# A hybrid encoder trunk on one core: the state-space branch written right behind its projection, beside the last gate

## The chip, the cores and the metric

The kernel runs on one core of one Trainium2 chip. The core has five engines, each with its own queue: TensorE (PE) for matmuls, VectorE (DVE) and ScalarE (ACT) for elementwise work, GpSimd (POOL) and SyncE (SP), which here mostly issue DMAs. The metric is the device time of one execution in microseconds; lower is better.

## The reference, cut to what matters

Two layers, each on 1024 tokens of width 1024. One projection of the normalised input feeds four branches of width 256:

- A, a convolution module: gated linear unit, causal depthwise convolution with 31 taps, LayerNorm, swish, a 256 by 256 matmul.
- B, a gated linear recurrence in chunks.
- C, a state-space branch: a causal convolution with 4 taps on x, B and C (768 columns), then a chunked scan:

```python
xbc = silu(causal_depthwise_conv(xbc, conv_w, conv_b))
a_cs = cumsum(a, axis=chunk)                     # a = dt * -exp(a_log)
scores = (C @ B.T) * masked_exp(causal, seg)     # seg: differences of a_cs
y = scores @ xdt + (C @ state) * exp(a_cs) + xs * d_skip
state = exp(a_cs_last) * state + B.T @ wx        # handed to the next chunk
y = rms_norm(y * silu(z))
```

- D, latent attention: a projection to a query latent (256), a key/value latent (128) and a rotary key (32), norms, up-projections, block-causal softmax.

A and D are multiplied by a SiLU gate of their own, B and C too (C's is z). One 1024 by 1024 output projection, a norm and the residual close the layer.

## The kernel before, in words

Matmuls of the large projections run in a two-part float32 format: each operand is split into a high and a low part ("wh"/"wl" for weights, "hh"/"hl" for the input), and each product is three matmuls (lines 209 to 211, 220 to 226, 347 to 349).

Each piece of a layer is a Python generator ("thread") that writes some instructions and yields how many units of work they were. The table PLAN gives each thread a start, an end and a total on a common scale; `weave` (line 262) always advances the thread whose position on that scale is lowest:

```python
def pos(self):
    return self.start + self.span * self.done / self.total
...
t = min(threads, key=Thread.pos)
w = next(t.gen, None)
```

So PLAN decides only the order in which instructions are written, and the numbers in it are places in that order, not times of the chip. The framework then lays out each engine's queue: an instruction that is written earlier goes first, but one whose inputs are there may pass earlier ones that are still waiting. Each engine then works through its queue in order. Tiles come from pools with a fixed number of slots per tag; a tile that finds no free slot waits for the release of an earlier one. The tags that matter here:

- `smA`, 2 accumulators of one bank: the gates' `psg` and `psgA`, the convolution tail's `ptA`, `pt2A`, `pyA`, and the state update `pstC` of branch C (line 31, 115 to 117). `smB`, 2: `ptx`, `pcb`, `pyC` of C, `pq` and `ptq` of the queries. `big`, 2 of two banks: `psx` (projection of x, B, C), `psd` and `pk` of D.
- `blk`, 19 slots of 128x544: x, B, C after their convolution hold 12 of them (6 per half of the tokens), the convolution of A holds 4 (`ca`), D wants 16 (`kT` 8, `cqT` 4, `vD` 4).
- `t2k`, 4 slots: `gtA` of the last gates, `lm` of C, later `pT` of attention. `t15`, 2 slots: `cn`, `kk` of D and `qk` of the queries. `k4`, 7 slots: gate tiles `gl`, `hnA`, `hsA`, and two of D's weight parts. Weights pass through `raw` (2 slots, DMAs from SP), `wh` and `wl` (3 each).

The threads around the change, for the first layer (keys end in 0; the second layer's end in 1):

- `x0`, th_x (line 700): projection of x, B, C in feature layout, then the 4-tap convolution on DVE (line 719) and SiLU (line 720).
- `ca0`/`cb0`, th_conv (line 473): branch A's 120 tap instructions on DVE (line 481), the first 57 on one line of the plan, the other 63 on another.
- `at0`, th_atail (line 485): its LayerNorm by transposes, pointwise matmul (line 515) and gate.
- `gd0`, gate_f(9, 1) (line 338): D's gate, four groups of 24 matmuls into `psgA`, each closed by a SiLU on ACT (line 353) and a DMA to DRAM.
- `c0`, th_c (line 724): branch C, eight chunks of 128 tokens. A chunk loads its decay row `lm` by a DMA from POOL (735), adds the mask (736), takes four exponentials on ACT (738), transposes (742), makes `pcb` (753), multiplies it into `lm` (754), makes `pyC` (760, 764) and hands the state on through `pstC` (774 to 778). Two chunks' halves end in a norm (789) and a DMA (365).
- `d0`, th_d (line 797): D's projection and keys, eight rows from the last token block to the first. A row is 24 matmuls into `psd`, a copy, three transposes (832), `pk` (841), scaling, four transposes (854) and copies to `kT`.
- `q0`: the first two query rows. Attention (`att0`) and the loading of the output weights (`w0`, line 948) are written after D's end; the output weights take the space of the layer's input, which is free once D's last `psd` is done.

The order in the trace is: B's levels, x's projection, D's gate, then C, A's tail and D's rows together, then attention and the output projection.

Of the kernel before, what the change touches and what calls it, by code (L numbers as in the profile page):

```python
# [47 lines left out]
    "fq0": (60.4, 110.8, 41),  # L48
    "dt0": (104, 115.8, 9),
    "ca0": (53.6, 123, 57),  # L50
    "cb0": (123, 300.5, 63),
    "gb0": (138.1, 155.9, 21),
    "b0": (123.3, 232.4, 120),
    "ga0": (151.5, 181.4, 21),
    "gc0": (203.4, 226.9, 21),
    "gd0": (278.8, 298.3, 21),
    "x0": (220.7, 257, 61.5),
    "at0": (296.3, 363.8, 22),
    "c0": (293.2, 362.4, 48.2),
    "d0": (283.6, 373.2, 72),  # L60
    "q0": (357.3, 375.6, 2),
    "o0": (482.2, 511, 8.2),
    "rot0": (221.2, 266.5, 1),
# [4 lines left out]
    "fq1": (59, 99.6, 41),  # L68
    "dt1": (104, 115.8, 9),
    "ca1": (57, 110, 44),  # L70
    "cb1": (110, 284.5, 76),
    "gb1": (117.9, 137.7, 21),
    "b1": (102.3, 200.5, 120),
    "ga1": (130.9, 155.3, 21),
    "gc1": (203.4, 230.3, 21),
    "gd1": (261.8, 280.6, 21),
    "x1": (212.9, 255.7, 61.5),
    "at1": (278.6, 342, 22),
    "c1": (275.5, 340.6, 48.2),
    "d1": (266.1, 351.4, 72),  # L80
    "q1": (335.5, 349.5, 2),
    "o1": (479.4, 508.2, 8.2),
    "att1": (347.1, 481.6, 144.8),
# [1084 lines left out]
```

## Time and profile before

| | us |
|---|---|
| median of three runs | 1263.75 (1263.0 to 1267.15) |
| the profiled execution, its own time | 1263.69 |
| its span in the trace | 1261.9 |
| PE busy | 1197.7 (95%) |
| DVE busy | 836.2 (66%) |
| ACT busy | 478.5 (38%) |
| chain that ended last, share of PE | 76% |
| chain that ended last, share of DVE | 14% |

Busy time of PE counts a matmul until its modelled end; a matmul that follows at once starts before that end. So a PE that is shown as busy may still be waiting a little between matmuls.

### The profile page before, as it was taken

The page shows a single profiled execution, that of the slowest core. Times are in us where ns is not written, and L with a number is a line of the kernel's source. Part 1 is how long each engine was busy: PE and PEld are TensorE (multiplying, and loading weights), DVE is VectorE, ACT ScalarE, POOL GpSimd, SP SyncE. Part 2 cuts the span into 40 slices and gives each one's busy share as a digit, 9 for nine tenths or more (in the row PEclk, how much of TensorE's full clock was granted, in tenths as well). Part 3 has the DMA queues.
Part 4 walks back from the last instruction along what each step waited for, and adds up shares of the span by engine and source line. Part 5 has one row for each costly group of instructions (what it writes and reads, how often), then busy time and mean ns, then how long its engine had stood idle before and what let it go on. Part 6 is the DMA issues. An engine that isn't in the chain of part 4 may idle for free.

```text
span 1261.9 us, 17853 instructions
## 1 busy us (share of the span) xinstructions
PE 1197.7 (95%) x6902; PEld 987.0 (78%) x6902; DVE 836.2 (66%) x1579; ACT 478.5 (38%) x1088; POOL 183.1 (15%) x290
## 2 busy tenths in 40 slices
PE   5999999899989989999999999998999998999997
PEld 5988899888878746678898889897888776566886
DVE  5566999985376386745454859999754763867232
ACT  5413322233474374433432222321435644644211
POOL 2100011201133111210020001211012322112000
PEclk9999999999999989989999999998999899999999
DMA  7001122201151040244221111211114311202531
GB/s 274 34 34 68 44 83 85 76 34 48 62 156 61 22 153 23 66 148 147 101 97 67 34 51 59 92 52 67 35 61 123 106 36 54 93 18 68 188 129 71
DMA packets 38660, 101.47 MB, mean 80 GB/s; under 512 B 5440, under 2 KB 13808, under 8 KB 38576
## 3 DMA queue, kind: packets, MB, share of 16 engines
q1 hardware_dynamic: 22848, 51.42, 11.9%
q0 software_dynamic: 14864, 46.04, 11.1%
q10 hardware_dynamic: 864, 2.88, 0.6%
q8 instruction: 54, 0.88, 0.3%
q14 instruction: 30, 0.25, 0.1%
HBM read 75.37 MB, written 25.20 MB: 80 GB/s over the span
## 4 chain that ended last, share of the span: by engine, by line
PE 76%; DVE 14%; ACT 3%; DMA 3%; issue 2%; POOL 0%; DVEq 0%; POOLq 0%; ACTq 0%
PE pz L991 13%; PE psx L220 4%; PE psx L223 4%; PE psx L226 4%; PE psc L909 3%; DVE ca L481 3%; PE plB L625 2%; PE psA L220 2%; PE psA L223 2%; PE psA L226 2%; PE poD L927 2%; PE ptp L923 2%; PE psgA L347 2%; PE psgA L348 2%; PE psgA L349 2%
## 5 line engine op out<-in xcount | busy, mean ns | idle before, releaser
L481 DVE SCALAR_TENSOR_TENSOR ca<-hpad,col,ca 128x512 f32<-128x512 f32 x240 | 186.3, 782 | 3.9
L176 DVE TENSOR_TENSOR wl<-raw,wh 128x1024 fp32r<-128x1024 f32 (+2 forms) x56 | 66.9, 1195 | 92.0 <-ACT wh L160 91.9
L160 ACT CAST wh<-raw 128x1024 fp32r<-128x1024 f32 (+2 forms) x56 | 57.5, 1027 | 139.8 <-PE psA L223 33.7
L991 PE MATMUL pz<-woh,yh 128*128 128x512 f32 x240 | 78.2, 405 | 0.2 <-ACT yh L160 0.2
L991 PE MATMUL pz<-woh,yl 128*128 128x512 f32 x240 | 75.7, 397 | 0.0
L991 PE MATMUL pz<-wol,yh 128*128 128x512 f32 x240 | 75.7, 397 | 0.0
L209 PE MATMUL psg<-wh,hh 128*128 128x256 f32 x256 | 73.9, 289 | 1.5 <-ACT gt L160 1.4
L909 PE MATMUL psc<-kT,qTt 96*128 96x512 f32 (+4 forms) x192 | 73.2, 505 | 0.9 <-ACT pe L914 0.8
L210 PE MATMUL psg<-wl,hh 128*128 128x256 f32 x256 | 73.2, 286 | 0.0
L211 PE MATMUL psg<-wh,hl 128*128 128x256 f32 x256 | 72.8, 284 | 0.0
L914 ACT ACTIVATE pe<-psc,nm 128x1024 f32<-128x1024 f32 (+7 forms) x64 | 47.2, 739 | 64.3 <-DVE nm L912 63.8
L625 PE MATMUL plB<-qz,krb 128*128 128x128 f32 x448 | 63.0, 288 | 8.5 <-DVE krb L635 8.5
L625 PEld LDWEIGHTS plB<-qz,krb 128*128 128x128 f32 x448 | 58.3, 200 | 10.7 <-issue 5.5
L220 PE MATMUL psx<-hh,wh 128*128 128x512 f32 x192 | 62.3, 403 | 0.0
L719 DVE SCALAR_TENSOR_TENSOR xbc<-xpad,col,xbc 128x512 f32<-128x512 f32 x72 | 51.1, 748 | 16.3 <-ACT xbc L172 15.5
L223 PE MATMUL psx<-hl,wh 128*128 128x512 f32 x192 | 61.7, 401 | 0.0
L226 PE MATMUL psx<-hh,wl 128*128 128x512 f32 x192 | 61.1, 397 | 0.0
L991 PEld LDWEIGHTS pz<-wol,yh 128*128 128x128 f32 x240 | 45.6, 190 | 10.6
L176 DVE TENSOR_TENSOR yl<-yt,yh 128x512 fp32r<-128x512 f32 x16 | 11.0, 690 | 64.7 <-ACT yh L160 64.7
L912 DVE TENSOR_REDUCE nm<-psc 128x1 f32<-128x1024 f32 (+7 forms) x64 | 47.2, 745 | 9.9 <-PE psc L909 9.9
L991 PEld LDWEIGHTS pz<-woh,yl 128*128 128x128 f32 x240 | 45.3, 189 | 10.6 <-issue 0.2
L991 PEld LDWEIGHTS pz<-woh,yh 128*128 128x128 f32 x240 | 44.9, 190 | 9.8 <-ACT yh L160 0.4
(331 smaller groups left out, 3052.3 us busy)
## 6 DMA issues: line engine op xcount, KB each, us to landing
raw<-in_w_dram SPq DMA_DIRECT2D x44, 512.0 KB, 3.4
rawo<-in_wo_dram SPq DMA_DIRECT2D x16, 512.0 KB, 4.1
gsp<-gt POOLq DMA_DIRECT2D x16, 256.0 KB, 2.5
gl<-gsp POOLq DMA_DIRECT2D x8, 512.0 KB, 5.0
gspF<-gtA POOLq DMA_DIRECT2D x16, 256.0 KB, 2.3
ysp<-gl POOLq DMA_DIRECT2D x8, 512.0 KB, 3.4
lm<-acsp POOLq DMA_DIRECT2D x16, 256.0 KB, 4.0
yt<-ysp SPq DMA_DIRECT2D x16, 256.0 KB, 3.4
```

The lines of the kernel that those rows point to most:

```text
L160: (V.tensor_copy if name in ONV else A.copy)(out_, in_)
L176: V.tensor_tensor(lo, src, hi.bitcast(F32), op=ALU.subtract)
L209: T.matmul(ps[:, :n], a, hs[k], start=(k == 0), stop=False)
L210: T.matmul(ps[:, :n], a, ls[k], start=False, stop=False)
L211: T.matmul(ps[:, :n], b, hs[k], start=False, stop=(k == KD - 1))
L220: T.matmul(ps[:, h * 512:(h + 1) * 512], w, hh[:, k, h * 512:(h + 1) * 512], start=(k == 0), stop=False)
L223: T.matmul(ps[:, h * 512:(h + 1) * 512], w, hl[:, k, h * 512:(h + 1) * 512], start=False, stop=False)
L226: T.matmul(ps[:, h * 512:(h + 1) * 512], wl, hh[:, k, h * 512:(h + 1) * 512], start=False, stop=(k == KD - 1))
L481: V.scalar_tensor_tensor(t, hp[:, k:k + 512], w[k], t, op0=ALU.mult, op1=ALU.add)
L625: T.matmul(pl[:, o0:o0 + P].rearrange("p (r b u) -> p r b u", r=2, u=u), k_[:, t_ * P:(t_ + 1) * P], z[:, :, t_ * P:(t_ + 1) * P].rearrang ...
L909: T.matmul(psc[:, c0:c1_], qTt[0:k_, h, :], kT[h, c0 // 512][0:k_, 0:c1_ - c0], start=True, stop=True)
L991: T.matmul(pz[n], a[:, k, :], w[:, k, n * 512:(n + 1) * 512], start=(k == 0 and a is yh and w is wh), stop=(k == KD - 1 and a is yl))
```

## The change

Ten lines of PLAN, five per layer; no generator is touched. On the plan's scale, x ends at 257 in the first layer and 255.7 in the second, before and after. C's start moves from 293.2 to 260 and from 275.5 to 258; D's gate starts at 268 (was 278.8) and 256 (was 261.8); the end of A's convolution moves from 300.5 to 285 and from 284.5 to 272; A's tail starts 9.3 and 4.6 places earlier; D's projection starts 4.4 and 3.9 places later and ends where it did.

```diff
-    "cb0": (123, 300.5, 63),
+    "cb0": (123, 285, 63),
-    "gd0": (278.8, 298.3, 21),
+    "gd0": (268, 292, 21),
-    "at0": (296.3, 363.8, 22),
-    "c0": (293.2, 362.4, 48.2),
-    "d0": (283.6, 373.2, 72),
+    "at0": (287, 358, 22),
+    "c0": (260, 350, 48.2),
+    "d0": (288, 373.2, 72),
...
-    "cb1": (110, 284.5, 76),
+    "cb1": (110, 272, 76),
-    "gd1": (261.8, 280.6, 21),
+    "gd1": (256, 278, 21),
-    "at1": (278.6, 342, 22),
-    "c1": (275.5, 340.6, 48.2),
-    "d1": (266.1, 351.4, 72),
+    "at1": (274, 336, 22),
+    "c1": (258, 334, 48.2),
+    "d1": (270, 351.4, 72),
```

## Rows read from the trace of the kernel before

**Rows 1.** The page, part 1: busy time, share of the span and instructions by engine.
```profile
PE 1197.7 (95%) x6902; PEld 987.0 (78%) x6902; DVE 836.2 (66%) x1579; ACT 478.5 (38%) x1088; POOL 183.1 (15%) x290
```

**Rows 2.** Windows, first layer, from gate D's start: length, busy by engine, clock, DMA.
```profile
326.02:349.22 23.20, 23.20 (x103) 19.04 (x102) 6.99 (x9) 10.68 (x17) 4.33 (x8) 1.00 0.26 80
349.22:375.00 25.78, 22.12 (x143) 19.00 (x142) 20.69 (x59) 21.79 (x64) 8.04 (x13) 1.00 0.55 177
375.00:415.70 40.70, 38.55 (x231) 32.37 (x230) 28.03 (x97) 18.65 (x69) 12.81 (x21) 1.00 0.15 47
415.70:440.23 24.53, 22.42 (x121) 19.12 (x120) 5.79 (x27) 8.23 (x31) 3.31 (x6) 1.00 0.08 28
440.23:452.00 11.77, 7.78 (x22) 4.27 (x21) 9.43 (x23) 9.11 (x22) 5.14 (x5) 0.74 0.40 118
```

**Rows 3.** Windows, second layer, behind gate D.
```profile
970.40:996.00 25.60, 23.07 (x132) 19.67 (x131) 20.43 (x58) 20.14 (x56) 8.04 (x13) 0.87 0.55 179
996.00:1038.60 42.60, 40.65 (x242) 34.19 (x241) 28.24 (x97) 20.45 (x78) 12.18 (x20) 1.00 0.14 45
```

**Rows 4.** Timeline of PE inside gate D: start, length, line, tiles.
```profile
340.37 0.40 PE L347 MATMUL psgA<-hh,wh 128*128 128x512 f32 x1
340.61 0.40 PE L348 MATMUL psgA<-hl,wh 128*128 128x512 f32 x1
```

**Rows 5.** Timeline of PE, rows of C, D and the first query, in time order.
```profile
353.99 1.00 PE L760 MATMUL pyC<-xdt,lm 128*128 128x64 f32 x8
...
358.65 1.08 PE L760 MATMUL pyC<-xdt,lm 128*128 128x64 f32 x8 [0.58 <-DVE mvA L495]
...
424.16 1.11 PE L841 MATMUL pk<-kvt,ckT 128*128 128x512 f32 x2 [0.47 <-DVE kr L850]
...
432.05 1.12 PE L841 MATMUL pk<-kvt,ckT 128*128 128x512 f32 x2 [0.92 <-ACT kT L160]
433.01 0.60 PE L879 MATMUL ptq<-idn,qk 128*96 128x128 f32 x4
433.45 0.61 PE L753 MATMUL pcb<-xbc,xbc 128*128 128x128 f32 x4
```

**Rows 6.** Timeline of ACT: a gate's SiLU, a table load, D's last weights, a query.
```profile
331.81 0.60 ACT L353 ACTIVATE gtA<-psgA 128x512 f32<-128x512 f32 x1 [0.33 <-PE psgA L349]
...
339.11 1.28 ACT L1082 ACT_TABLE_LOAD   x1
340.40 1.28 ACT L738 ACTIVATE lm<-lm,nacs 128x128 f32<-128x128 f32 x4
...
352.76 0.89 ACT L160 CAST wh<-raw 128x832 fp32r<-128x832 f32 x1 [1.50 <-DMA raw<-in_wd_dram]
...
430.42 0.58 ACT L166 ACTIVATE qk<-pq,rq 128x384 f32<-128x384 f32 x1
```

**Rows 7.** Timeline of POOL: two of the four loads of D's first keys' mask rows.
```profile
331.49 0.53 POOL L811 DMA_DIRECT2D kT<-in_amask_dram  x1 [9.60 <-ACT xbc L720]
...
361.32 0.59 POOL L811 DMA_DIRECT2D kT<-in_amask_dram  x1
```

**Rows 8.** The page, part 6: DMA issue, count, size, median us to landing.
```profile
lm<-acsp POOLq DMA_DIRECT2D x16, 256.0 KB, 4.0
```

**Rows 9.** Windows of line 481 alone (A's taps), DVE busy and count.
```profile
60.00:240.00 180.00, 77.24 (x101) 1.00 0.17 61
...
680.00:860.00 180.00, 70.94 (x93) 1.00 0.17 61
```

**Rows 10.** Windows ahead of x's projection, both layers, as in Rows 2.
```profile
240.00:250.00 10.00, 6.41 (x46) 5.89 (x45) 10.00 (x17) 4.34 (x8) 0.72 (x1) 0.90 0.25 79
860.00:870.00 10.00, 5.48 (x22) 4.95 (x23) 10.00 (x17) 1.45 (x4) 0.71 (x1) 0.62 0.37 133
```

**Rows 11.** Timeline of DVE at D's end, first layer.
```profile
448.11 1.23 DVE L789 TENSOR_TENSOR gl<-gl,msc 128x1024 f32<-128x1024 f32 x1 [1.32 <-POOL msc L147]
...
450.39 0.28 DVE L160 COPY kT<-pk 96x128 f32<-96x128 f32 x1
```

## The prediction, made before the result was known

> **What bounds the kernel now.** I read the page's busy times first, then windows of each layer from gate D to attention, then the timelines of PE, ACT, POOL and DVE inside them. PE is busy for 95% of the span [rows 1], so no edit of the order can save much; what an order can change is the time in which PE has nothing to do. In the first layer [rows 2] gate D is solid: 23.20 us, PE idle 0, DVE 6.99 us and ACT 10.68 us busy. Behind it, where C, A's tail and D's rows run together, PE is idle for 25.78 - 22.12 = 3.66 us and then 40.70 - 38.55 = 2.15 us; in D's last rows 24.53 - 22.42 = 2.11 us; and at D's end 11.77 - 7.78 = 3.99 us with the clock at 0.74. The second layer repeats it [rows 3]: 2.53 us idle and 1.95 us, and in the first of these stretches the mean granted clock is 0.87. A clock that is either full (2.4 GHz) or half (1.2 GHz) and means 0.87 was at half for 26% of 25.60 us, 6.7 us, which takes away up to 3.3 us of PE.
>
> These idle times are a little too small: a gate matmul is drawn 0.40 us long and the next starts 0.24 us after it [rows 4], so each time PE runs dry some 0.16 us are hidden. With about ten such holes a layer that is 1.6 us more per layer, an estimate.
>
> What makes the holes is that three threads start cold at the same moment, right behind the gate: each is a chain across PE, DVE and ACT, and they wait for slots too. Of D's first four key tiles one is loaded at 331.49 us, after POOL waited 9.60 us for x's last SiLU to free a slot, and one only at 361.32 us [rows 7], when A's tail had given slots back. D's last weight part is cast at 352.76 us, 3.5 us behind the gate's end, having waited for its load [rows 6].
>
> **The change, part by part.** Its work is the same: no instruction is added but table loads, and each DMA is issued once as before. So I price waits.
>
> *C ahead of and beside gate D.* Written places: of gate D's 21 units 16 stood before C's first chunk; now three chunks stand among them in the first layer (from 260, 11.2 places a chunk, the gate ending at 292), two in the second. C needs x's last SiLU, so it can't run before about 332 us, but there it now goes first. PE pays for it in the gate: a 128-wide matmul takes (433.45 - 433.01) / 4 = 0.11 us [rows 5], a chunk has 24, so 2.6 us, some 8 us for three chunks. That lengthens the gate's stretch and shortens what follows by as much: zero by itself. What is won: of the 12 `blk` slots that x, B and C hold, 6 are given back after chunk 3, now earlier than D's rows want them, and behind the gate only two chains are cold instead of three. What stays is D's last weights, which will again be late by about 3.5 us, since their slots are freed by the gate's last group. The holes ahead of D's last rows come to 3.66 + 2.15 + 2.53 + 1.95 = 10.3 us, with 3.3 us of clock and 3.2 us hidden 16.8 us; bounds 0 and -16.8; I take half, -8.4, because the chain and slot half of them goes and the late weights and D's own waits stay.
>
> *The gate's accumulators.* This is the wait that is added. `smA` has two slots, handed out in written order; in the first layer C's state update `pstC` now stands before the gate's first group, and again before the third. One slot is thus held for C until x is through, and the gate's second group waits for the first group's SiLU: 0.33 + 0.60 us [rows 6], three times at most in the first layer and once in the second, 3.7 us. Behind the waiting matmul on PE stand only matmuls of C, which are written between. They fill most of it; I take +0.5 (bounds 0 and the third rival's +11).
>
> *ACT.* C's exponentials and the gate's SiLUs use different tables; the load takes 1.28 us and the exponential starts at its end, 340.40 against 339.11 + 1.28 [rows 6]. Two or three more alternations a layer make 5 to 8 us on an engine that was busy for 10.68 of 23.20 us, in a stretch that grows by 8 us: hidden, 0; without that cover it would land in the gate's hand-over and belongs to the third rival. The Trainium skill (ScalarE: Activation LUTs, What ACT_TABLE_LOAD costs) adds a drain of about 1.38 us to every switch, 2.66 us in all. This trace shows no such gap behind the load; by the skill's figure the alternations would cost 5 to 8 us at 2.66 / 1.28 times, 11 to 16 us of ACT; the stretch, 31 us with C's matmuls, still covers that, so the sum stays, and the gate's hand-over would be the more at risk.
>
> *A's convolution ends earlier.* It moves 3 to 4 taps of about 0.77 us [rows 9] ahead in the order, while B's chain makes PE wait 3.6 and 4.5 us [rows 10]. But the taps already run ahead of their place: 101 of 120 are done at 240 us [rows 9], and the 101st stands at place 244 before and 234 after, both behind B's end at 232; in the second layer the 93rd, done at 860 us, stands at 220 and 212, behind 200.5. They only fill gaps of DVE in both orders. I take 0; at worst 4 x 0.77 per layer, +6 in all.
>
> *A's tail a little earlier, D later.* POOL is passed by C's gate load, `lm` loads and zeroing of the state, which now go before D's key rows instead of behind the 9.60 us wait [rows 7]; SP keeps its order (x, gate, D). A's tail gives its `blk` slots back when the gate's last group frees `smA`, about as before: 0 (bounds -1 and +1).
>
> *D's last rows.* C's end moves from 362 to 350 while D ends at the same place, so D's last rows have less beside them. A row alone takes 432.05 - 424.16 = 7.89 us, with 0.47 or 0.92 us of waiting before `pk` [rows 5]. Two rows were nearly alone in the stretch with 2.11 us idle [rows 2], 1.06 us each, and with 0.16 us hidden at each of a row's two waits about 1.3 us; I count half a row more per layer, +1.3 (bounds 0 and two rows each, +5.2).
>
> *D's end.* C's eighth chunk was stuck: its `pcb` runs at 433.45 us, right behind the first query's `ptq`, which was written before it and held the place in `smB` until the query's scaling at 430.42 us found a slot of `t15` [rows 5, 6]. So C's last norm, 1.23 us on DVE, stood at 448.11 us in front of a copy of `kT` [rows 11] for which attention waits. Now C's end is written before the queries and is gone from there: -1.2 per layer, I take -2.1 in all (bounds 0 and -2.5).
>
> The sum: -8.4 + 0.5 + 0 + 0 + 0 + 1.3 - 2.1 = -8.7 us on the profiled execution's 1263.69, 1255.0 us. That execution equals the median shown (1263.75) within 0.1 us. I call a difference under 0.3%, 3.8 us, no change.
>
> **The rivals.** *The work is only moved* (no change). Gate D had no hole in PE, so the 8 us of C's matmuls now fill nothing there and are missing as filler later. For it: the total of matmuls is fixed, and D alone loses 1.3 us a row. Against it: the holes stood where all three threads were present, so filler wasn't what lacked. With two rows a layer more alone (+5.2) and a quarter of the holes closed (-4.2): -4.2 + 0.5 + 5.2 - 2.1 = -0.6: 1263.
>
> *All holes close* (more gain). The clock stays up in the second layer and the chains overlap wholly: -16.8 + 0.5 + 1.3 - 2.1 = -17: 1247. For it: C's fastest chunk takes 358.65 - 353.99 = 4.7 us [rows 5], less than a gate group (23.20 / 4 = 5.8 us). Against it: the late weights.
>
> *The gate waits for C* (slower). `smA` again: gate group 3 stands behind chunk 1's `pstC`. If a chunk needs its `lm` load (4.0 us [rows 8]), mask, table load and exponentials (1.28 + 1.28 us) one after the other, and the table is taken back for each SiLU (1.28), a chunk takes over 8 us against the gate's 5.8, and PE stops in the gate. It decides from the point where chunk 1's state update ends later than the gate's second group, some 13 us behind x's last SiLU. Price: hand-overs 3.7, then about 5 us of standing in the first layer and 2 in the second, 11 in all, less 2.1 at D's end: +9, 1273. Against it: the first two `lm` tiles have slots before the gate's own and can be ready ahead of x's end. The Trainium skill (Perfetto Trace Analysis, Optimization Strategy) reads a repeated gap on the saturated engine as too few slots for the next tile; gate D shows no such gap before, so this would be new.
>
> **How the numbers follow.** Forecast 0.50; only moved 0.21; all holes 0.12; gate waits 0.17. Faster: 0.50 + 0.12 = 0.62; same 0.21; slower 0.17. The forecast's own range is 1250 to 1259. The whole range goes down to 1244, past the all-holes case, and up to 1269, half-way into the slow one, which leaves out about 0.05 below and 0.12 above.
>
> **What would show it.** Right: in gate D's stretch PE stays busy with `ptx`, `pcb`, `pyC` of the first chunks between `psgA` groups, the fourth key row's load is issued before 355 us instead of at 361.32, the second layer's clock behind the gate is 1.00, and no norm of C stands behind D's end. Wrong: idle time of PE in front of `psgA` with the SiLU or the state update as releaser; holes of equal size in the stretch behind the gate; three or more D rows alone; or more than 3.6 and 4.5 us of idle PE ahead of x's projection, which would mean that A's taps do cost.

## The result, and the profile after

| | kernel before | changed kernel |
|---|---|---|
| median of four runs each, us | 1264.92 (1263.0 to 1267.15) | 1280.78 (1279.92 to 1281.77) |
| the profiled execution, us | 1263.69 | 1280.68 |
| its span, us | 1261.9 | 1278.5 |

The changed kernel is slower: ratio 1.0136, 95% interval 1.0118 to 1.0153. I had forecast 1255.0. The work is the same but for six more table loads on ACT; part 1 of the page after, against [rows 1]:

```profile
PE 1202.3 (94%) x6902; PEld 988.9 (77%) x6902; DVE 839.1 (66%) x1579; ACT 487.8 (38%) x1094; POOL 180.5 (14%) x290
```

PE is busy 4.6 us longer and the span is 16.6 us longer. Where that went is read best from one number per stage, which I work out from the matmuls of the trace: the length of a stretch less the sum, over its matmuls, of the spacing at which matmuls of that line and shape follow each other at full clock (the spacing that 15% of them undercut in the kernel before; 0.229 us for 512 columns, 0.109 for 128). It holds idle time, the holes hidden under drawn lengths, and what a halved clock takes. I call it lost time. The stages are cut at B's first level, x's first and last matmul, the gate's last, the last matmul of D's projection into `psd` and the last scores of attention. Each row is one profiled execution. e1 has no row, for its profiled execution took 4126.73 us; of its trace only the order on PE is used.

```
lost us of PE       first layer                          second layer
kernel            B..x     x  gate     D  attn    |   B..x     x  gate     D  attn
before            11.2   3.5   0.3  12.4  31.6    |   15.6   4.2   0.4  14.2  32.6
changed           12.8   4.4   8.2  11.4  36.7    |   16.9   5.1   0.7  11.6  37.0
e2  gate first    11.9   3.5   1.1  18.8  34.4    |   16.9   5.3   0.7  13.0  34.6
e3  taps back     12.4   3.5   9.1  11.6  36.3    |   16.9   4.2   0.7  11.6  34.5
e4  C's end back  13.0   4.7   3.0  18.0  32.4    |   16.9   4.0   0.7  12.0  31.6
e5  fifth cast    12.9   4.5   8.2  11.4  35.7    |   16.9   5.1   0.7  11.9  33.7
e6  mask of x     11.1   3.7   7.5  12.7  35.4    |   16.3   4.2   0.7  11.6  34.6
e7  e2 and k4     13.3   4.3   1.1  14.6  36.9    |   17.4   3.8   0.7  10.8  36.7
e8  C as before   11.2   3.6   0.2  24.3  31.8    |   15.6   3.8   0.4  16.2  34.3
e9  C alone       13.5   4.3  12.1  13.7  37.1    |   16.9   5.2   1.8  12.5  35.4
e10 e8, A back    11.1   3.5   0.2  18.4  31.6    |   15.6   5.1   0.4  15.7  37.3
e11 all repairs   11.1   3.8   0.2  16.2  32.0    |   16.2   4.1   0.7  12.5  31.6
e12 layer 2 only  11.1   3.6   0.3  14.4  31.5    |   15.6   3.9   0.7  12.7  31.6
e13 gate alone    11.0   3.9   0.2  19.0  33.0    |   15.6   4.3   0.4  16.7  33.0
e14 D alone       11.1   3.7   0.2  14.8  31.7    |   15.6   4.7   0.4  14.6  33.4
```

The kernel before loses 126.0 us in these ten stages, the changed one 144.8. That is 18.8 us, 2.2 more than the spans differ by; 1.6 of this lies ahead of B's first level, which the changed kernel reached earlier. The difference has three places and one gain: the first layer's gate +7.9; attention +5.1 and +4.4; B's end and x's projection +2.5 and +2.2; and D's stage -1.0 and -2.6. How far such a number scatters is seen in two kernels. e12's first layer has exactly the queues of the kernel before on all five engines: D's stage reads 14.4 there and 12.4 before, the other stages agree within 0.1. e3 has the queues of the changed kernel from end to end, and its second layer's attention reads 34.5 against 37.0, the ten stages 140.8 against 144.8.

**The gate.** Windows of the first layer after, cut at x's end and the gate's first and last matmul, then a stretch behind the gate and D's last rows, in the columns of [rows 2] (length, busy by engine, clock, DMA):

```profile
326.90:338.30 11.40, 6.53 (x31) 5.46 (x30) 7.75 (x14) 4.59 (x9) 1.04 (x2) 0.72 0.11 39
338.30:364.20 25.90, 25.90 (x129) 21.67 (x129) 7.61 (x18) 8.94 (x22) 3.27 (x6) 0.99 0.18 52
364.20:390.00 25.80, 21.57 (x137) 18.37 (x136) 20.85 (x62) 18.84 (x57) 10.48 (x16) 1.00 0.47 153
425.00:449.30 24.30, 22.18 (x111) 18.10 (x109) 6.91 (x30) 8.92 (x34) 5.24 (x8) 1.00 0.12 45
```

In the first row PE is idle for 4.9 of 11.4 us and the clock means 0.72. Timeline of PE there:

```profile
333.37 0.80 PE L753 MATMUL pcb<-xbc,xbc 128*128 128x128 f32 x2 [2.88 <-ACT xbc L720]
334.95 1.97 PE L760 MATMUL pyC<-xdt,lm 128*128 128x64 f32 x8 [0.78 <-DVE lm L754]
336.71 1.06 PE L742 MATMUL ptx<-idn,xbc 128*128 128x128 f32 x4
337.57 1.09 PE L774 MATMUL pstC<-xdt,btk 128*128 128x128 f32 x4
338.31 0.65 PE L347 MATMUL psgA<-hh,wh 128*128 128x512 f32 x1
```

The gate's first matmul starts at 338.31 us, right behind C's first state update `pstC`, although nothing that it reads was late (in e2, below, it starts before x has ended) and both slots of `smA` had been free since before x's projection. In front of it PE waited 2.88 us for x's last SiLU and went on at the lower clock: `pyC` takes 1.97 us where it took 1.00 in [rows 5]. In the second layer the written order puts two of the gate's groups ahead of the first state update, the gate starts at x's end, and PE has no holes in it:

```profile
961.80:990.40 28.60, 28.52 (x146) 23.88 (x145) 12.58 (x23) 15.34 (x29) 4.87 (x9) 1.00 0.23 71
990.40:1016.00 25.60, 22.15 (x135) 18.48 (x134) 20.98 (x65) 19.52 (x60) 8.18 (x15) 1.00 0.48 151
```

**Attention's start.** ACT at the first exponentials; before and then after. L160 and L955 on `woh` are casts of the output weights, L914 is attention's exponential.

```profile
449.58 1.04 ACT L160 CAST woh<-rawo 128x1024 fp32r<-128x1024 f32 x1
450.70 0.42 ACT L160 COPY kT<-pk 96x128 f32<-96x128 f32 x2
451.15 1.28 ACT L1082 ACT_TABLE_LOAD   x1
453.77 1.11 ACT L914 ACTIVATE pe<-psc,nm 128x1024 f32<-128x1024 f32 x1 [1.34 <-DVE nm L912]
...
455.12 1.15 ACT L955 ACTIVATE woh<-rawo,col 128x1024 fp32r<-128x1024 f32 x1
```

```profile
458.37 1.04 ACT L160 CAST woh<-rawo 128x1024 fp32r<-128x1024 f32 x1 [0.96 <-DMA rawo<-in_wo_dram]
459.32 0.42 ACT L160 COPY kT<-pk 96x128 f32<-96x128 f32 x2
461.88 1.15 ACT L955 ACTIVATE woh<-rawo,col 128x1024 fp32r<-128x1024 f32 x1 [2.14 <-DMA rawo<-in_wo_dram]
463.04 1.28 ACT L1082 ACT_TABLE_LOAD   x1
464.34 1.11 ACT L914 ACTIVATE pe<-psc,nm 128x1024 f32<-128x1024 f32 x1
```

Before, four casts stand ahead of the table load and the fifth (L955) behind the first exponential. After, the fifth stands in front of it and waits 2.14 us for its load. From D's last `psd` to the first exponential it takes 453.77 - 440.4 = 13.4 us before and 464.34 - 449.5 = 14.8 after, and the clock then stays low. The window of 7 us from the first exponential on, before and then after:

```profile
453.80:460.80 7.00, 6.37 (x34) 3.28 (x34) 5.72 (x6) 6.04 (x9) 0.54 (x1) 1.00 0.50 191
```

```profile
464.30:471.30 7.00, 5.70 (x15) 3.53 (x16) 3.60 (x4) 5.00 (x8) 0.00 (x0) 0.55 0.45 150
```

**B's end.** DVE and then PE inside B's last levels, first of the kernel before and then after. L634 and L635 make `qz` and `krb`, for which PE's `plB` waits; L481 is a tap of A, L176 a part of a weight, L736 C's mask.

```profile
242.22 0.41 DVE L635 TENSOR_TENSOR krb<-krb,totB 128x256 f32<-128x256 f32 x1
242.55 0.74 DVE L481 SCALAR_TENSOR_TENSOR ca<-hpad,col,ca 128x512 f32<-128x512 f32 x1
243.22 1.22 DVE L176 TENSOR_TENSOR wl<-raw,wh 128x1024 fp32r<-128x1024 f32 x1
244.35 0.68 DVE L634 TENSOR_TENSOR qz<-qz,totB 128x512 f32<-128x512 f32 x1
245.42 1.16 PE L625 MATMUL plB<-qz,krb 128*128 128x128 f32 x8 [1.51 <-DVE krb L635]
```

```profile
240.53 0.42 DVE L635 TENSOR_TENSOR krb<-krb,totB 128x256 f32<-128x256 f32 x1
240.87 0.75 DVE L481 SCALAR_TENSOR_TENSOR ca<-hpad,col,ca 128x512 f32<-128x512 f32 x1
241.93 0.69 DVE L736 TENSOR_TENSOR lm<-lm,negb 128x512 f32<-128x512 f32 x1 [0.31 <-DMA lm<-acsp]
242.54 1.22 DVE L176 TENSOR_TENSOR wl<-raw,wh 128x1024 fp32r<-128x1024 f32 x1
243.67 0.68 DVE L634 TENSOR_TENSOR qz<-qz,totB 128x512 f32<-128x512 f32 x1
244.75 1.16 PE L625 MATMUL plB<-qz,krb 128*128 128x128 f32 x8 [2.44 <-DVE krb L635]
```

C's mask stands in DVE's queue in front of the next `qz`: from `krb` to `qz` it takes 2.13 us before and 3.14 after. A second mask, at 245.82 us, adds 0.60 in the same way, and together that is the 1.6 us which this stage loses more. In the second layer a mask at 874.52 us takes 0.6 of the 1.3 us, and the rest is one tap of A (0.67 us) that stands one place earlier on DVE; C's move put it there, since the stage loses the same 16.9 us in e9 (below), where A's lines are untouched.

On ACT C's exponentials (L738) follow the masks:

```profile
241.72 1.05 ACT L160 CAST wh<-raw 128x1024 fp32r<-128x1024 f32 x1
242.79 1.28 ACT L1082 ACT_TABLE_LOAD   x1
244.08 1.28 ACT L738 ACTIVATE lm<-lm,nacs 128x128 f32<-128x128 f32 x4
```

Masks and exponentials run here, some 85 us before x's last SiLU, because their inputs are there early. In the kernel before neither a table load nor an exponential of C stands between 237 and 258 us. ACT itself is not what PE waits for: in the second layer it is idle for 4.53 us between C's exponentials and its next copy.

### The profile page after: what moved, and what is told of

Its sections match the earlier page's. It is cut to its first block, busy times and chain, and to the rows that moved or that the text cites. A ratio compares the mean times of both kernels' runs of the same rounds, so it can differ in the third digit from the quotient of the medians.

```text
span 1278.5 us, 17857 instructions
## 1 busy us (share of the span) xinstructions
PE 1202.3 (94%) x6902; PEld 988.9 (77%) x6902; DVE 839.1 (66%) x1579; ACT 487.8 (38%) x1094; POOL 180.5 (14%) x290
## 3 DMA queue, kind: packets, MB, share of 16 engines
q10 hardware_dynamic: 864, 2.88, 0.6%
## 4 chain that ended last, share of the span: by engine, by line
PE 45%; DVE 5%; ACT 3%; issue 1%; DMA 1%; DVEq 0%; ACTq 0%
PE pz L991 11%; PE psc L909 2%; PE psx L220 2%; PE psx L223 2%; PE psx L226 2%; PE ptp L923 1%; PE plB L625 1%; PE poD L927 1%; DVE ca L481 1%; PE psA L220 1%; PE psA L223 1%; PE psgA L348 1%; PE psgA L347 1%; PE psA L226 1%; PE psgA L349 1%; PE psd L209 1%
## 5 line engine op out<-in xcount | busy, mean ns | idle before, releaser
L481 DVE SCALAR_TENSOR_TENSOR ca<-hpad,col,ca 128x512 f32<-128x512 f32 x240 | 186.5, 783 | 3.9
L176 DVE TENSOR_TENSOR wl<-raw,wh 128x1024 fp32r<-128x1024 f32 (+2 forms) x56 | 67.0, 1196 | 72.2 <-ACT wh L160 72.0
L160 ACT CAST wh<-raw 128x1024 fp32r<-128x1024 f32 (+2 forms) x56 | 57.5, 1027 | 133.2 <-PE psA L223 33.7
L909 PE MATMUL psc<-kT,qTt 96*128 96x512 f32 (+4 forms) x192 | 77.4, 530 | 1.7 <-ACT kT L160 1.7
L914 ACT ACTIVATE pe<-psc,nm 128x1024 f32<-128x1024 f32 (+7 forms) x64 | 47.3, 741 | 69.6 <-DVE nm L912 69.0
L912 DVE TENSOR_REDUCE nm<-psc 128x1 f32<-128x1024 f32 (+7 forms) x64 | 47.1, 746 | 16.3 <-PE psc L909 16.1
L909 PEld LDWEIGHTS psc<-kT,qTt 96*128 96x128 f32 (+1 forms) x192 | 35.3, 207 | 26.3 <-issue 20.3
L923 PE MATMUL ptp<-idn,pe 128*128 128x128 f32 x288 | 48.4, 294 | 7.5 <-ACT pe L914 7.3
L923 PEld LDWEIGHTS ptp<-idn,pe 128*128 128x128 f32 x288 | 34.6, 148 | 25.3 <-issue 11.4
L176 DVE TENSOR_TENSOR yl<-yt,yh 128x512 fp32r<-128x512 f32 x16 | 11.0, 690 | 65.7 <-ACT yh L160 65.7
```

The source lines that it names most:

```text
L176: V.tensor_tensor(lo, src, hi.bitcast(F32), op=ALU.subtract)
L481: V.scalar_tensor_tensor(t, hp[:, k:k + 512], w[k], t, op0=ALU.mult, op1=ALU.add)
L909: T.matmul(psc[:, c0:c1_], qTt[0:k_, h, :], kT[h, c0 // 512][0:k_, 0:c1_ - c0], start=True, stop=True)
L923: T.transpose(ptp[:, (j - j0) * P:(j - j0 + 1) * P], pes[r][:, j * P:(j + 1) * P], idn)
```

## The experiments

The ratios are to the kernel before, measured on the same chip in the same hours; the changed kernel's is 1.0136.

**e1, e2, e9: what stands in front of the gate.** e1 gives the gate other accumulators, e2 moves one line of PLAN, e9 is the kernel before with C's two lines changed.

```diff
e1  -                    ps = sm("psgA")
    +                    ps = big("psgD")[:, 0:512] if b == 1 else sm("psgA")
e2  -    "gd0": (268, 292, 21),
    +    "gd0": (256, 280, 21),
e9  -    "c0": (293.2, 362.4, 48.2),  "c1": (275.5, 340.6, 48.2),
    +    "c0": (260, 350, 48.2),      "c1": (258, 334, 48.2),
```

> The changed kernel (1280.8 us) with D's gate put into the two double-bank accumulators of tag big, which x's projection has just left, instead of smA; nothing else is changed. Theory (the gate stands in PE's queue behind C's first state update, because both take their accumulators from smA and the update is written first): the first layer's gate starts within 1 us of x's last matmul, near 327 us instead of 338.3, the stretch from 320 to 340 us loses none of its 8 us of PE time, and the total falls by 7 to 12 us, to 1269 to 1274; attention's longer start (+4.4 and +3.2 us) stays as it is. Rival (C's vector and activation work itself delays D, wherever the gate's accumulators are): the gate starts earlier but its SiLUs wait, D's projection starts as late as now, and the total stays within 4 us of 1280.

Measured: 1272.36 us, ratio 1.0076 (1.0048 to 1.0105), as the theory said. PLAN is the same as in the changed kernel, but the order on PE is another (`psgD` is the gate):

```profile
1064.83 1.16 PE L753 MATMUL pcb<-xbc,xbc 128*128 128x128 f32 x2
1065.43 1.24 PE L347 MATMUL psgD<-hh,wh 128*128 128x512 f32 x1
...
1122.22 3.12 PE L760 MATMUL pyC<-xdt,lm 128*128 128x64 f32 x8
```

45 matmuls of the gate now stand ahead of the second half of `pcb`, in front of which the changed kernel waits for x's last SiLU, and 88 ahead of the first `pstC`. So it was `smA`, handed out in written order, that put the gate behind the state update.

> The changed kernel with one line moved: the first layer's D gate is written 12 places earlier (256 to 280 instead of 268 to 292), so that its first two groups stand ahead of C's first state update; accumulators as they are. The second layer is left alone. Theory of the queue position: the gate starts at about 327 us, and the total falls by 7 to 10 us, to 1271 to 1274, all of it in the first layer. Rival (C's work beside the gate delays D anyway): within 4 us of 1280. If e1 gains clearly more than this one, the hand-overs of smA further back in the gate cost too, beside the position of its first group.

Measured: 1279.41 us, ratio 1.0131 (1.0098 to 1.0165). The gate started at 327.3 us, and its stage lost 1.1 us instead of 8.2. But the time hardly fell: D's stage now lost 18.8 us instead of 11.4. The position was right as the reason for the hole, and mending it alone did not give back the time. I had written that if e1 gained clearly more than e2, the hand-overs of `smA` cost too. e1's median is 7 us lower and the intervals overlap only from 1.0098 to 1.0105, so that reading stays open beside the one that follows.

> The kernel before with C's two lines alone changed (260 to 350 and 258 to 334); the gate, A's convolution, A's tail and D stay where they were. In this order two state updates of C stand ahead of the first layer's gate in PE's queue, not one, and five output-weight casts stand ahead of attention's first exponential in both layers. Theory (C's move is what costs, by the gate's position behind the state update and by attention's start): the first layer's gate stage loses 14 to 20 us of PE against 0.3 before, attention's stages lose 3 to 5 us more each, and the total is 1280 to 1290. Rival (the other eight lines cost, as e8 suggests, and C's move by itself is harmless): 1261 to 1266.

Measured: 1286.72 us, ratio 1.0184 (1.0159 to 1.0209). Two state updates of the first layer stand ahead of the gate in this queue, and both run first:

```profile
341.41 1.09 PE L774 MATMUL pstC<-xdt,btk 128*128 128x128 f32 x4
...
347.78 1.06 PE L774 MATMUL pstC<-xdt,btk 128*128 128x128 f32 x4
348.49 0.77 PE L347 MATMUL psgA<-hh,wh 128*128 128x512 f32 x1
```

x had ended at 330.9. With none, one and two updates ahead the gate's stage loses 0.3, 8.2 and 12.1 us (before, changed, e9; I had written 14 to 20 for the last); attention and B's end cost here what they cost in the changed kernel. So C's move alone is enough for all three losses.

**e7: where e2's gain went.** Behind e2's gate a chunk's mask came late. POOL, then DVE, then PE of e2:

```profile
365.44 1.06 POOL L735 DMA_DIRECT2D lm<-acsp  x2 [6.95 <-DMA gspF<-gtA]
369.89 0.69 DVE L736 TENSOR_TENSOR lm<-lm,negb 128x512 f32<-128x512 f32 x1 [3.38 <-DMA lm<-acsp]
372.73 0.68 PE L753 MATMUL pcb<-xbc,xbc 128*128 128x128 f32 x4 [4.62 <-DVE xsd L780]
```

`lm` and the gate's results `gtA` share the four slots of `t2k`. POOL waited 6.95 us for a `gtA` to be written out before it could issue the next load of `lm`; DVE's mask waited 3.38 us for that load, with a release of `smB` queued behind it, and PE stood for 4.62 us in front of `pcb`. e7 keeps the gate's results in two tiles of `k4`:

```diff
+                gt2 = k4("gtA2") if b == 1 else None
...
-                    gt = tmp(512, "gtA")
+                    gt = gt2[:, m * 512:(m + 1) * 512] if b == 1 else tmp(512, "gtA")
```

> The kernel of e2 (first layer's gate written first, 1279.4 us), in which D's gate also stores its SiLU results in tag k4 (two tiles of 4 KB) instead of the four slots of t2k that C's decay rows lm need. In e2 the gate started in time, but 10 us were lost behind it, where the mask of a chunk waited 3.4 us for lm's load, which POOL had issued 7 us late, after waiting for a slot. Theory (C beside the gate is limited by the slots of t2k that it shares with the gate's results): PE's lost time from the gate's end to D's last matmul falls from 18.8 to about 12 us in the first layer, and the total to 1271 to 1274; more masks of C run ahead of x, which may cost another 1 us there. Rival (the chain PE, DVE, ACT of C's chunks itself, or DVE's load): that lost time stays at 17 to 19 us and the total at 1277 to 1281.

Measured: 1274.55 us, ratio 1.0101 (1.0083 to 1.0118). D's stage loses 14.6 us, next to the 12.4 and 14.4 of the old order, and B's end loses a little more, both as the theory had it; the time is a hair above its range, and its interval overlaps that of e2, so the gain is likely but not clear of the noise.

**e4, e5: attention's start.** e4 puts C's end back, which leaves matmuls of C at D's end and brings the order of four casts; e5 makes the last four casts wait for attention's first row maximum.

```diff
e4  -    "c0": (260, 350, 48.2),      "c1": (258, 334, 48.2),
    +    "c0": (260, 362.4, 48.2),    "c1": (258, 340.6, 48.2),
e5  +                        if "g" not in wo_t:
    +                            wo_t["g"] = small(4, "gq", 1)
    +                            V.tensor_scalar(wo_t["g"], nm.to_broadcast([P, 4]), 0.0, None, op0=ALU.mult)
    +                            V.tensor_tensor(wo_t["g"], wo_t["g"], col[:, C_BG:C_BG + 4], op=ALU.add)
    ...
    -                    gc = col[:, C_BG + YB[k] - 2:C_BG + YB[k] - 1]
    +                    gc = wo_t["g"][:, YB[k] - 2:YB[k] - 1]
```

> The changed kernel with C's end put back to its old places (362.4 and 340.6) while its start stays at the new ones, both layers; nothing else is changed. In this order four output-weight casts stand ahead of attention's first exponential on ACT, as before, where the changed kernel has five. Theory (attention starts slowly because the fifth cast, which waits for its load, stands in front of the first exponential, and because PE has no matmuls of C left at D's end, so that the clock falls to half): attention's stages lose their 4.4 and 3.2 us, the clock is 1.00 within 8 us of the first scores, and the total falls by 5 to 8 us, to 1273 to 1276; the gate still starts at 338 us. Rival (attention's start is late only because all before it is late): attention's stages stay at 90.5 and 90.7 us, and the total within 2 us of 1280.8.

Measured: 1270.18 us, ratio 1.0064 (1.0044 to 1.0083): more than forecast. Attention's lost time is back at 32.4 and 31.6 us. One thing I had wrong: the gate started at 331.5 us, since in this order, too, its first group stands ahead of the first state update. That closed most of the hole in the gate (3.0 us lost), but D's stage took it back (18.0), as in e2; so the fall in time comes from attention. (The profiled execution took 1274.40 us, so these stages account for 6 of the 10.6 us that the medians differ by.)

> The changed kernel, in which the last four output-weight casts read their scale from a small copy that is made behind attention's first row maximum (two extra DVE instructions on 128x4 per layer); so the fifth cast can no longer stand in front of attention's first exponential on ACT. Nothing else is changed, and C's matmuls are still gone from D's end. Theory (the fifth cast is what delays attention's start): PE's lost time from the first scores to 25 us behind them falls from 9.8 us to about 7 in both layers, the rest of attention by another 1, and the total falls by 6 to 9 us, to 1271 to 1274. Rival (it is the missing filler at D's end and the clock that falls with it): the stretch keeps 9 to 10 us of lost time, and the total stays within 2 us of 1280.

Measured: 1278.42 us, ratio 1.0124 (1.0102 to 1.0145). That is the rival's time, and the interval holds the changed kernel's ratio. The 25 us from the first scores on lose 10.0 us in the first layer, as the rival said, and 8.0 in the second; before they lose 6.6 and 7.7, in the changed kernel 9.8 and 9.8. Attention as a whole loses 1.0 and 3.3 us less than in the changed kernel, but only 0.6 and 0.8 less than in e3, which has the changed kernel's queues. So holding the fifth cast back gave nothing clear of the scatter. The held casts now stand in pairs between the next exponentials on ACT.

The order of the casts goes with the loss over all kernels: with four casts ahead of the first exponential and then one between exponentials attention loses 31.5 to 33.4 us; with four and then pairs 33.0 to 35.7; with five 34.4 to 37.3. e10's second layer speaks against the other reading: its C lines are those of before, so C's matmuls stand at D's end, and with five casts it still loses 37.3 us:

```profile
1084.78 1.15 ACT L955 ACTIVATE woh<-rawo,col 128x1024 fp32r<-128x1024 f32 x1 [2.79 <-DMA rawo<-in_wo_dram]
1085.94 1.28 ACT L1082 ACT_TABLE_LOAD   x1
1087.24 1.12 ACT L914 ACTIVATE pe<-psc,nm 128x1024 f32<-128x1024 f32 x1
```

There the fifth cast waited 2.79 us for its load, with the table load and the first exponential behind it. The missing filler at D's end adds little: D's end to the first scores loses 6.1 us instead of 5.3 in the changed kernel's first layer. So e4 shows that C's earlier end is what costs attention; that it does so by the casts is argued from these rows, not shown by a run that changes the casts alone.

**e3, e6: B's end.** e3 puts A's taps back (300.5 and 284.5); e6 makes C's mask depend on x's last SiLU:

```diff
+            negx = br.tile([P, P], BF16, tag="negx", name="negx", bufs=1)
+            V.scalar_tensor_tensor(negx, xbc[4][0][:, 0:P], 0.0, negb, op0=ALU.mult, op1=ALU.add)
...
-                    V.tensor_tensor(lm, lm, negb.unsqueeze(1).to_broadcast([P, 4, P]), op=ALU.add)
+                    V.tensor_tensor(lm, lm, negx.unsqueeze(1).to_broadcast([P, 4, P]), op=ALU.add)
```

> The changed kernel with the end of A's convolution put back to its old places (300.5 and 284.5) in both layers; nothing else is changed. If the earlier taps take DVE from B's chain, x's projection starts 0.1 us later in the first layer's case and 1.3 us earlier in the second layer's, and the total falls by 2 to 4 us, to 1277 to 1279. My prediction's own step says 0: within 1 us of 1280.8.

Measured: 1279.3 us, ratio 1.0129 (1.0094 to 1.0165). B's end loses 12.4 and 16.9 us, as in the changed kernel. The trace says why: the two kernels have the same instructions in the same order on PE, DVE, ACT and POOL. Beside the other eight lines these two move no tap, so they cost nothing, and e3 is a second sample of the changed kernel.

> The changed kernel, in which C's mask is a copy that is made from x's last SiLU (one extra DVE instruction of 128x128 per layer, the mask's values unchanged), so that no mask or exponential of C can stand on DVE and ACT inside B's last levels, at 242 and 874 us; they follow x's end instead. Theory (C's masks and exponentials, with their table loads, take ACT and DVE from B's chain): PE's lost time from B's start to x's projection goes back from 12.8 and 16.9 us to 11.2 and 15.6, and the total falls by 2 to 3 us unless C's first chunk then waits for its mask. Rival (A's taps or the execution's own scatter): lost time stays at 12.5 and 16.9 and the total within 1 us of 1280.

Measured: 1276.22 us, ratio 1.0106 (1.0085 to 1.0128). B's end loses 11.1 us as before and 16.3, x's projection 3.7 and 4.2 instead of 4.4 and 5.1: 3.9 us together. B's end gets back all of its loss in the first layer and half (0.6 of 1.3) in the second, which is what the masks took on DVE. x's projection can't be counted: with C's masks still early it reads 3.5 in the first layer of e2 and e3 and 3.8 to 4.2 in the second of e3, e4 and e7. C's first chunk waited no longer than in the changed kernel (0.78 us in front of `pyC`).

**e8, e10, e13, e14: the other lines.** Each leaves C where it was. e8 is the changed kernel with C's lines back; e10 has A's tail back too; e13 and e14 are the kernel before with one thread moved.

```diff
e8   changed kernel, with "c0": (293.2, 362.4, 48.2), "c1": (275.5, 340.6, 48.2)
e10  e8, with "at0": (296.3, 363.8, 22), "at1": (278.6, 342, 22)
e13  kernel before, with "gd0": (268, 292, 21), "gd1": (256, 278, 21)
e14  kernel before, with "d0": (288, 373.2, 72), "d1": (270, 351.4, 72)
```

> The changed kernel with only C's two lines put back (293.2 to 362.4 and 275.5 to 340.6): A's convolution, A's tail, D's gate and D's projection stay where the change has put them. If C's move alone is the cause, everything goes back: 1262 to 1265 against 1262.6 for the kernel before. If the other eight lines cost too (taps, A's tail, D's later start), 1266 to 1270. If they gain, under 1261.

Measured: 1276.99 us, ratio 1.0122 (1.01 to 1.0143): none of the three. The other eight lines without C cost nearly as much as all ten, and in another place: D's stage loses 24.3 us in the first layer.

> The kernel of e8 (C's lines as before, 1277.0 us) with A's tail also put back (296.3 to 363.8 and 278.6 to 342); so of the change only the gate, the convolution's end and D's start are left. In e8 D's stage lost 24.3 us of PE in the first layer (12.4 before), with one wait of 3.7 us for the SiLU of A's tail, whose table was loaded and taken away twice by C's exponentials. Theory (A's tail, when it is moved ahead of C, is what costs in e8): D's stage loses 12 to 14 us again, and the total is 1262 to 1266. Rival (D's later start or the earlier gate): it loses over 20 us, and the total is 1273 to 1278.

Measured: 1274.97 us, ratio 1.0083 (1.0059 to 1.0107): the rival's time, with D's stage between the two. Of that stage's loss A's tail explains about half, 24.3 to 18.4. The other half is the gate's line or D's. (The time is held up by the second layer's attention, which has five casts here.)

> The kernel before with D's gate alone at its new places (268 to 292 and 256 to 278). In e10, where C and A's tail stand as before and only the gate, the convolution's end and D's start are changed, D's stage still lost 18.4 us of PE in the first layer against 12.4. In the queue of this kernel three chunks of C follow each other without the 24 matmuls of a D row between them, where the kernel before has a row between. Theory (the gate's move changes where D's first rows stand among C's chunks, and the chunks lose their filler): D's stage loses 17 to 20 us, attention of the first layer 2 more (two casts stand together between its exponentials), and the total is 1268 to 1273. Rival (D's later start is what costs): D's stage loses 12 to 14 us, the total is within 2 us of the kernel before.

> The kernel before with D's projection and keys alone at the new places (288 to 373.2 and 270 to 351.4). PE's queue differs only in that six matmuls of D's first row stand behind half of the gate and not behind a quarter of it. Theory (the gate's move is what costs in e10): the stages lose what they lose before, and the total is within 2 us of the kernel before. Rival (D's later start costs): D's stage loses 17 to 20 us in the first layer, and the total is 1267 to 1272.

Measured: the gate alone 1275.36 us, ratio 1.0089 (1.0061 to 1.0118), D's stage 19.0 us; D alone 1266.5 us, ratio 1.0024 (1.0006 to 1.0041), D's stage 14.8. So it is the gate's line, though its time came out above the range; D alone missed both of its ranges, 3.3 us above the kernel before. The window of e13 behind the gate, against the second of [rows 2]:

```profile
351.20:377.00 25.80, 21.11 (x115) 18.32 (x113) 20.09 (x56) 19.11 (x55) 7.71 (x13) 0.80 0.54 169
```

In its queue the chunks of C follow each other without the 24 matmuls of a D row that stand between two of them in the kernel before; the clock means 0.80 where it was 1.00. That the missing row is what costs is read from the order; no run tests it by itself.

**e11, e12: repaired versions.** e11 joins e2's gate line, e4's end of C and e6's mask. e12 has the first layer of before, and in the second the changed lines with C's end at 340.6 and the mask of e6.

> The changed kernel with three repairs together: the first layer's gate written first (256 to 280), C's end at its old places (362.4 and 340.6), and C's mask made from x's last SiLU as in e6. Four casts stand ahead of attention's first exponential in both layers. If the three causes that I see (gate behind the state update, attention's start, masks inside B) are what the change costs, the sum is, against before: first layer gate +1, D's stage +4 to +6 (the slots of lm remain), attention 0 to +1; second layer -2 to -3; the total 1263 to 1267. If there is another cause, 1270 or more.

Measured: 1264.75 us, ratio 1.0009 (0.9995 to 1.0023). The three repairs take back what the change cost; the interval reaches no further than 0.23%. D's stage of the first layer still loses 16.2 us; the slots of `lm` are as they were.

> The first layer as before; in the second layer all changed lines, with C's end at its old place (340.6) and C's mask made from x's last SiLU. In the second layer two of the gate's groups stand ahead of C's first state update anyway, and the stages between x's end and D's end lost 12.3 us of PE in the changed kernel against 14.6 before. Theory (C beside the gate gains where it doesn't hold the gate up): faster than before by 2 to 4 us, 1258 to 1260 against 1262. Rival (what is gained there is lost at attention's start): within 1 us of before.

Measured: 1261.92 us, ratio 0.9987 (0.9972 to 1.0003). Neither of my two figures came out, and the gain that I expected is not shown: the interval holds no change. It was the only version with a time below that of before.

## Why the prediction was wrong

By the stages the terms came out so: the gate +8.2 us against +0.5, attention's start +9.5 where *D's end* had -2.1, D's stage -3.6 against -8.4, and B's end, which no term had for C, +2.9.

The step that failed first is *the gate's accumulators*, +0.5. I had seen that `smA` is handed out in written order and that `pstC` is written ahead of the gate's first group. I then priced it as slot hand-overs further back in the gate and wrote "Behind the waiting matmul on PE stand only matmuls of C". It is the other way round. What stands behind C's waiting matmuls in PE's queue is the gate, which could run at once: it started 11.4 us late, and the gate's stage lost 7.9 us more than before. Its rival *The gate waits for C* had the direction and a price of 11, but put the wait at the gate's third group and tied it to chunk 1's state update being late; here chunk 0's stood ahead of the first group, and both slots were free. The Trainium skill (PSUM — Partial Sum Buffer, Engine vs sequencer instructions) states that matmuls start and complete in program order; the row at 338.31 agrees, and I had not applied it to the work behind the wait. e9 and e1 show the mechanism; e2 shows that a gate that starts in time need not win the 7.9 us back. C beside the gate then runs into the slots of `t2k`, which I had not priced; how much of e2's loss that is stays open, since e1 shares these slots too and gained.

The second failure is *D's end*, -2.1. The norm did go from there (it stands at 428.84 us now), but nothing was won: D's end to the first scores loses 6.1 us against 5.3. I looked only at what leaves the stage, not at what moves up: with C gone, a fifth output-weight cast stood ahead of attention's first exponential, and attention lost 9.5 us more in the two layers. No rival had this; it is the largest term. That C's end is the cause is shown by e4, that the cast is the way is likely.

*C ahead of and beside gate D*, -8.4: D's stage lost 1.0 and 2.6 us less, so 3.6, and the 1.0 is within the scatter. The second layer behaved as I wrote: the clock behind the gate is 1.00 where it was 0.87 [rows 3], and the second layer's gate has C's matmuls between its groups without a hole. The first layer did not: the fourth `kT` load came at 366.69 us, not before 355.

*ACT*, 0: right. In the second layer's gate the tables change three times (the third load is at 986.75 us), and PE is idle for 0.08 of 28.60 us:

```profile
977.92 1.28 ACT L1082 ACT_TABLE_LOAD   x1
979.21 1.28 ACT L738 ACTIVATE lm<-lm,nacs 128x128 f32<-128x128 f32 x4
...
982.88 1.28 ACT L353 ACT_TABLE_LOAD   x1 [1.80 <-issue]
```

What I left out is that C also runs ahead of x, inside B's last levels, and there it is the mask on DVE that costs, not the exponentials on ACT: 1.6 us of B's end in the first layer and 0.6 in the second. I had worked out that C "can't run before about 332 us"; its masks and exponentials need nothing of x. My sign for costly taps came with it, PE idle for 4.78 us from 240 to 250 us where it was 3.6 [rows 10], and pointed at the wrong cause. The drain of about 1.38 us that the Trainium skill (ScalarE: Activation LUTs, What ACT_TABLE_LOAD costs) adds to a switch is not there: the load at 242.79 us begins at the end of the cast (241.72 + 1.05), and the exponential at 244.08 at the end of the load.

*A's convolution*, 0: right, and for a simpler reason than mine, since its lines move nothing (e3). *A's tail a little earlier, D later*, 0: not visible in the changed kernel, but not harmless either. Without C's move, A's tail costs some 6 us in D's stage (e8, e10). *D's last rows*, +1.3: not seen; the stretch that holds the last of them, 425 to 449.3 us, idles for 2.12 us, as 2.11 before.

The changes do not add up. C alone costs 1.84%, the gate alone 0.89%, D alone 0.24%, all ten lines together 1.36%: by the table C's move fills what the gate's and A's moves open in D's stage, and opens holes in the gate, in attention and at B's end.

Open is how much of D's stage of the first layer in e11, 16.2 us, comes from the slots; a kernel with both repairs has five casts in its first layer and would not tell.

## What to carry to other kernels

When work that waits is written ahead of work that could run, look at what stands behind it in the same queue, whether or not a slot is short; the price can be the whole wait, not a hand-over. Ask of each moved thread which of its instructions need none of the inputs that hold the rest: those run far ahead of their place and meet the chain that is critical there, on whichever engine it runs. And when a thread ends earlier, read the queue of the next stage's first instructions: something else moves up into the room.

## What the runs showed that I had not expected

- Small edits of a written order are expensive on a kernel that has been balanced by hand: moving one gate by 11 and 6 places cost 0.89% (e13), and six matmuls of D's first row that stand behind half of the gate instead of a quarter of it, with a few instructions reordered at D's end in the second layer, go with 0.24% (0.06 to 0.41, e14).
- The same queues gave 12.4 and 14.4 us of lost time in D's stage (before, e12) and 37.0 and 34.5 in attention (changed, e3), and the stretch ahead of B's levels took from 138.0 to 142.0 us in the profiled executions of kernels that begin alike. A step of 2 us can't be read from a single trace.
- A table load of 1.28 us costs nothing where PE has matmuls that ACT doesn't feed: three of them in the second layer's gate, where PE idles for 0.08 us.
